# A product's difference of weight blocks, kept from its first use instead of loaded three times

## The chip, the core and the metric

The kernel runs on one NeuronCore of a Trainium2 chip. A core has five engines that run side by side, each through its own instructions in order: TensorE (PE, matrix products, results into PSUM banks), VectorE (DVE) and ScalarE (ACT) for elementwise work, GpSimd (POOL) and SyncE (SP), which here issues most transfers. Sixteen DMA engines move the data of all queues. Engines wait for one another through semaphores. The metric is the time of one execution on the device in microseconds; shorter is better.

## What is computed

One layer of a decoder trunk over 1024 positions of width 2048, cut to what matters:

```
h = RMSNorm(x)
P = h @ W_in                        # all columns of all groups in one projection
A: gMLP gating     B: gated DeltaNet (8 heads, short conv on q, k, v, chunked delta rule)
C: attention to 256 memory tokens   # each times SiLU of its own columns of P
x = x + concat(A, B, C) @ W_out
y = RMSNorm(x)
```

Everything is float32. A float32 product is made from three products of faster type: each operand is split into a high part and a rest, and high x high, high x rest and rest x high are added.

## The kernel before

**A planner sets the order.** The kernel's text doesn't issue its instructions at once. `Plan.add` (line 138) records each with its operands, a rank and the instructions it depends on. `Plan.issue` (line 229) then plays them through with the kernel's own fixed costs (for example a fixed latency for a transfer, line 67, and a further one for GpSimd's, line 204) and writes out an order for every engine: whatever is ready goes by rank, small numbers first, then by place in the program. So each engine's order, fixed before the program runs, follows from the whole list of instructions. `behind(op)` holds an instruction back until `op` is done. Matrix products of the projection have rank 9 and fill TensorE wherever nothing more urgent is ready; weight and operand loads have rank 4, splits into high part and rest have rank 2, subtractions of blocks rank 2 (`minus`, line 1397), the steps of the early inverse rank 3 (line 1280).

**Two parts of the projection.** The first half of the DeltaNet heads is projected plainly, head by head (`project`, line 861). The rest of P, and the output projection, use Strassen-Winograd products: a pair of 512 column blocks and the two halves of the positions make a 2x2 problem with the two halves of the 2048 rows of W, and seven products of blocks are made instead of eight (`seven`, line 1340). There are five column pairs of W_in (`pairs`, line 740; `project_pair`, line 1460) and two of W_out. Each product m is made in four chunks of two 128-row blocks; a chunk is 24 matmuls of 128x512 with two operands that are loaded, combined and split. The order of the products of a pair is 2, 1, 6, 5, 3, 7, 4 (line 1337).

**The operands.** The left ones (`h_left`, line 1378) are loaded from DRAM, sums and differences being made earlier. The right ones are made from weight blocks B(i, b): half i of the rows, column block b. With T = B(0,1) - B(0,0), product 1 takes B(0,0), product 6 takes B(1,1) - T, product 5 takes T itself, product 3 takes B(1,1) and turns the kept T into B(1,1) - T, and products 7 and 4 use that. `rights_made` (line 1430) does it. `plain` loads a pair of 128x512 blocks into one of three raw tiles (`wraw2`, line 1302; the trace calls them `wraw` or `y`), `load2` loads into given tiles. The tiles in which T is kept are eight of 128x512, two per chunk (`kept`, line 1305): slots of the rings that the trace calls kT, qT, kd and ai, which an earlier part of the DeltaNet work used.

**What runs beside the first pair.** The first column pair (C_Q and C_K of the later heads) starts when the plain projection ends. At the same time the DeltaNet work of the early heads goes on. It needs inverses of 32x32 triangular blocks (`inverse`, line 995): 62 small steps on VectorE and one copy, then GpSimd sends the result to DRAM (`tdrearly`, `udrearly`), reads it back in pieces into `tblk` and `ut` (`levels`, line 1022), and small matmuls combine the pieces. Then the scan over chunks follows, interleaved with the products.

**The first pair is an exception.** In `rights_made` the flag `late` is set for pair 0 alone. There the kept tiles aren't filled in product 1. Product 6 loads B(0,1) into two of the `yz` tiles and B(0,0) into a raw tile, and makes T in `yz`; product 5 loads both again and makes T in the kept tiles.

Of the kernel before, what the change touches and what calls it, by code (L numbers as in the profile page):

```python
# [22 lines left out]
HT = 512  # L23
# [37 lines left out]
class Plan:  # L61
# [27 lines left out]
    @contextmanager  # L89
    def rank(self, cls):  # L90
        old, self.cls = self.cls, cls
        yield
        self.cls = old

    @contextmanager
    def behind(self, op):
        old, self.gate = self.gate, op
        yield
        self.gate = old
# [204 lines left out]
def kernel(  # L304
# [115 lines left out]
    def main_bank():  # L420
        turn["acc"] += 1
        return acc[turn["acc"] % 2]
# [45 lines left out]
    def triple(a, l, r, start, stop, cls=9):  # L468

        mm(a, l[0], r[0], start, False, cls)  # L470
        mm(a, l[0], r[1], False, False, cls)
        return mm(a, l[1], r[0], False, stop, cls)
# [194 lines left out]
    for mt in range(2):  # L667
        t = [ring["ai"](F32R) for _ in range(2)]
# [9 lines left out]
    for h in range(NX):  # L678
        t = ring["vs"](F32R).rearrange("p (s m) -> p s m", s=2)
# [68 lines left out]
    def blk(w, k, c0):  # L748
        return w[k * P : (k + 1) * P, c0 : c0 + HT]
# [547 lines left out]
    yu, yz, obs = ([t[:, k * HT : (k + 1) * HT] for k in range(4)] for t in ywide[:3])  # L1297
# [7 lines left out]
    kept = [[ring[tag](slot=k) for k in range(2)] for tag in ("kT", "qT", "kd", "ai")]  # L1305
# [7 lines left out]
    wide = [main_bank(), main_bank()] + acc[2:4]  # L1313
# [3 lines left out]
    def load2(ts, src):  # L1317

        for i, x_ in enumerate(src):
            t = ts[i] if len(ts) == 2 else ts[0][:, i * HT : (i + 1) * HT]  # L1320
            Q.dma_start(t, x_)
        return ts
# [9 lines left out]
    def add(o, a, b, cls=1):  # L1332
        with rank(cls):
            V.tensor_tensor(out=o, in0=a, in1=b, op=ALU.add)


    ORDER, FIRST, SUM = (2, 1, 6, 5, 3, 7, 4), (1, 7, 2), {5: 0, 6: 1, 7: 2, 3: 3}
    ends, chunk_ends = {}, [marks[-1]] * 8

    def seven(left, right, banks, takes, order, rows=False, last=False):  # L1340


        for n, key in enumerate(order):
            c, m = divmod(key, 10)
            bank = banks(key)

            def product(t, i, a, w):
                for u in range(2):
                    mine, whole = slice(u * HT + t * P, u * HT + (t + 1) * P), slice(u * HT, (u + 1) * HT)
                    l, r, ls, rs = (a, w, mine, whole) if rows else (w, a, mine, whole)  # L1350
                    triple(bank[t], (l[0][:, ls], l[1][:, ls]), (r[0][:, rs], r[1][:, rs]),
                           i + u == 0 and m in FIRST, i + u == NH - 1)

            held = []
            for i in range(0, NH, 2):
                js = (i, i + 1)
                a, w = left(m, js), right[c](m, js)
                if last and key == order[-1] and i >= NH - 6:
                    held.append((i, a, w))
                else:  # L1360
                    for t in range(NT):
                        product(t, i, a, w)
                    chunk_ends.append(R.ops[-1])
                    if todo and len(chunk_ends) % 4 == 0:
                        with behind(R.ops[-1]), rank(3):
                            todo.pop(0)()
            for t in range(NT):
                for h in held:
                    product(t, *h)
                ends[key, t] = R.ops[-1]  # L1370
                takes[key](t, bank[t])
# [16 lines left out]
    def plain(srcs):  # L1388
        with rank(4):
            return load2([wraw2()], srcs)[0]  # L1390

    def split_r(srcs):
        return split2(srcs, whi3(), wlo3())
# [3 lines left out]
    def minus(o, a, b):  # L1397
        with rank(2):
            V.tensor_tensor(out=o, in0=a, in1=b, op=ALU.subtract)
# [27 lines left out]

        return get

    def rights_made(blocks, late=False):  # L1430

        def get(m, js):
            n = js[0] // 2
            ts = yz[n % 2 * 2 :][:2] if late and m == 6 else kept[n]
            if m in ((6, 5) if late else (1,)):
                with rank(4), behind(chunk_ends[-8]):
                    load2(ts, [blocks(0, 1, j) for j in js])
                if late:  # L1440
                    r = plain([blocks(0, 0, j) for j in js])
                    for i, t in enumerate(ts):
                        minus(t, t, r[:, i * HT : (i + 1) * HT])
            if m == 5:
                return split_r(ts)
            r = plain([blocks(*AT[m], j) for j in js])
            parts = [(t, r[:, i * HT : (i + 1) * HT]) for i, t in enumerate(ts)]
            if m < 4:
                w = split_r([r])
                if m == 3 or m == 1 and not late:  # L1450
                    for t, x_ in parts:
                        minus(t, *((t, x_) if m == 1 else (x_, t)))
                return w
            for t, x_ in parts:
                minus(x_, *((t, x_) if m == 7 else (x_, t)))
            return split_r([r])

        return get

    def project_pair(c, done, dest=None):  # L1460


        def keep(o, a):
            with rank(1):
                S.copy(o, a)

        def fin(hf, b, t, a, y=None):
            o = dest(hf, t) if dest and b == 1 else ob()
            if y is None:
                keep(o, a)  # L1470
            else:
                add(o, a, y)
            with rank(2.4):
                done(hf, b, t, o)

        takes = {
            2: lambda t, a: keep(yu[t], a),
            1: lambda t, a: fin(0, 0, t, a, yu[t]),
            6: lambda t, a: keep(yz[t], a),
            5: lambda t, a: keep(yu[t], a),  # L1480
            3: lambda t, a: fin(0, 1, t, a),
            7: lambda t, a: fin(1, 1, t, a, yu[t]),
            4: lambda t, a: fin(1, 0, t, a, yz[t]),
        }

        def w_block(i, b, j):
            return blk(w_in, NH * i + j, pairs[c][b])

        seven(h_left, [rights_made(w_block, c == 0)], lambda m: wide, takes, ORDER)

    def to_conv(which):
        def done(hf, t, y):
# [4 lines left out]
    def blocks(c, *dones, dest=None):  # L1497
        project_pair(c, lambda hf, b, t, y: dones[b](hf, t, y), dest)
# [145 lines left out]
    for n, (tag, to) in enumerate((("gt", mkT), ("inv", mv))):  # L1644
        for i in range(NX // 2):
            t = ring[tag](F32R).rearrange("p (h s m) -> p h s m", h=2, s=2)
# [106 lines left out]
    takes, rights = {}, []  # L1753

    def out_pair(cp):
# [42 lines left out]
        def w_block(i, b, j):  # L1798
            return blk(w_out, (set1, set2)[i][j], (c1 + b) * HT)

        rights.append((rights_made, rights_back)[cp](w_block))

    out_pair(0)
# [33 lines left out]
```

## Time and profile before

| | |
|---|---|
| runs | 1626.72 us median of 3 (1624.07 to 1627.04) |
| profiled execution | 1629.2 us, span of its instructions 1627.2 us |
| granted TensorE clock, mean | 0.997 |
| VectorE / ScalarE / GpSimd busy | 1268.3 / 1025.2 / 277.4 us |
| moved by DMA | 428.92 MB, mean 264 GB/s |

In the profile's rows all instructions carry line 300, since the planner issues them from there; work is told apart by tile names, which leave out buffer numbers (`y` is any of the tiles y0 to y3, among them `yz`, and the third raw tile). `out<-in,in` names what an instruction writes and reads. A row of waits reads: waiting engine and tile <- what ended the wait: total us, times, longest. A row of DMA issues ends in the count, the size of one, and the median us from issue to landing. A matmul that is shown as busy is pipelined with the next one: 24 matmuls of 128x512 follow one another at about 0.22 us.

### The profile page before, as it was taken

What the parts mean: (1) busy time and instruction counts of PE and PEld (TensorE: products, weight loads), DVE (VectorE), ACT (ScalarE), POOL (GpSimd) and SP (SyncE); (2) the same over time, 40 slices, a digit from 0 to 9 for tenths busy, and PEclk for the clock granted to TensorE, in tenths of its full rate; (3) what the DMA queues carried; (4) which work ended last, traced back from release to release, by engine and by line L of the source; (5) the groups of instructions that cost most, each with busy time, mean ns of one, the idle gap of its engine ahead of it and who ended that gap; (6) DMA issues with size and microseconds to landing.
All of it is one profiled execution on the core that took longest, in us unless ns stands there. A gap on an engine that the chain in (4) does not pass through costs nothing.

```text
span 1627.2 us, 26085 instructions
## 1 busy us (share of the span) xinstructions
PE 1611.0 (99%) x8576; PEld 1354.4 (83%) x8576; DVE 1268.3 (78%) x2119; ACT 1025.2 (63%) x2216; POOL 277.4 (17%) x466
## 2 busy tenths in 40 slices
PE   9999999999999999999999999999999999999997
PEld 8988888888888888888888888888888888888886
DVE  6866787869855567898998898778668888679875
ACT  7767675765456555888787444776757774345355
POOL 0011220360252210112222502223100000000001
PEclk9999999999999999999999999999999999999999
DMA  9866998888967975689868976898768879688646
GB/s 326 245 197 193 305 303 260 277 255 309 369 204 256 308 242 182 209 279 364 289 215 279 350 243 204 256 340 262 253 221 271 290 246 371 202 267 294 222 150 235
DMA packets 277129, 428.92 MB, mean 264 GB/s; under 512 B 30665, under 2 KB 102402, under 8 KB 276994
## 3 DMA queue, kind: packets, MB, share of 16 engines
q1 hardware_dynamic: 254098, 366.75, 68.5%
q0 software_dynamic: 22144, 59.40, 10.9%
q8 instruction: 67, 1.10, 0.3%
q10 hardware_dynamic: 752, 1.12, 0.2%
q14 instruction: 68, 0.56, 0.1%
HBM read 339.57 MB, written 87.06 MB: 262 GB/s over the span
## 4 chain that ended last, share of the span: by engine, by line
PE 88%; DMA 4%; issue 3%; DVE 3%; ACT 1%; SPq 0%; POOL 0%; POOLq 0%; DVEq 0%; ACTq 0%
PE acc L300 66%; PE dn L300 22%; DMA wraw<-hTd 1%; DVE y L300 1%; DMA wraw<-in_w_in_dram 1%; DMA tdrearly<-inv 0%; DVE alo L300 0%; DVE wlo L300 0%; DMA vs<-od 0%; DMA raws<-h0d 0%; ACT ahi L300 0%; DVE tn L300 0%; DMA qT<-in_mem_dram 0%; DMA ut<-udrearly 0%; DMA tblk<-tdrearly 0%
## 5 line engine op out<-in xcount | busy, mean ns | idle before, releaser
L300 PE MATMUL acc<-ahi,whi 128*128 128x512 f32 (+1 forms) x1512 | 537.6, 393 | 0.1
L300 PE MATMUL acc<-ahi,wlo 128*128 128x512 f32 (+1 forms) x1144 | 447.8, 392 | 0.0
L300 PEld LDWEIGHTS acc<-ahi,whi 128*128 128x128 f32 x1512 | 283.3, 188 | 53.9 <-ACT xr L300 0.2
L300 PE MATMUL acc<-alo,whi 128*128 128x512 f32 (+1 forms) x776 | 302.1, 389 | 0.0
L300 PEld LDWEIGHTS acc<-ahi,wlo 128*128 128x128 f32 x1144 | 215.6, 188 | 41.3 <-DVE wlo L300 0.5
L300 ACT CAST whi<-wraw 128x512 fp32r<-128x512 f32 (+1 forms) x167 | 133.9, 803 | 123.7 <-PE acc L300 90.6
L300 DVE TENSOR_TENSOR wlo<-wraw,whi 128x512 fp32r<-128x512 f32 (+1 forms) x167 | 153.7, 921 | 70.7 <-ACT whi L300 67.6
L300 ACT CAST ahi<-raws 128x1024 fp32r<-128x1024 f32 x130 | 136.3, 1048 | 64.0 <-PE acc L300 25.5
L300 PEld LDWEIGHTS acc<-alo,whi 128*128 128x128 f32 x776 | 146.4, 189 | 27.5
L300 PE MATMUL acc<-ahi,zl 128*128 128x512 f32 x376 | 149.1, 396 | 0.0
L300 PE MATMUL acc<-alo,zh 128*128 128x512 f32 x376 | 148.7, 395 | 0.0
L300 PE MATMUL acc<-ahi,zh 128*128 128x512 f32 x376 | 148.1, 394 | 0.0
L300 POOL TENSOR_TENSOR small<-small,mhalf 128x1 f32<-128x1 f32 x26 | 15.6, 605 | 531.2 <-DVE small L300 524.7
L300 DVE TENSOR_TENSOR alo<-y,ahi 128x1024 fp32r<-128x1024 f32 x65 | 79.4, 1221 | 15.0 <-ACT ahi L300 14.6
L300 ACT CAST ahi<-y 128x1024 fp32r<-128x1024 f32 x65 | 68.1, 1047 | 36.4 <-PE dn L300 18.3
L300 DVE TENSOR_TENSOR alo<-raws,ahi 128x1024 fp32r<-128x1024 f32 x65 | 79.8, 1228 | 13.9 <-ACT ahi L300 13.8
L300 DVE TENSOR_TENSOR ahi<-raws,ahi 128x1024 fp32r<-128x1024 f32 x65 | 79.4, 1221 | 13.2 <-ACT ahi L300 13.0
L300 PEld LDWEIGHTS acc<-alo,zh 128*128 128x128 f32 x376 | 70.7, 188 | 13.7
L300 PEld LDWEIGHTS acc<-ahi,zh 128*128 128x128 f32 x376 | 70.8, 188 | 13.6
L300 PEld LDWEIGHTS acc<-ahi,zl 128*128 128x128 f32 x376 | 70.8, 188 | 13.5
L300 PE MATMUL acc<-whi,ahi 128*128 128x512 f32 x232 | 79.9, 392 | 0.0
L300 PE MATMUL dn<-whi,ahi 128*128 128x512 f32 x216 | 74.2, 389 | 0.0
(423 smaller groups left out, 3397.6 us busy)
## 6 DMA issues: line engine op xcount, KB each, us to landing
wraw<-in_w_in_dram SPq DMA_DIRECT2D x268, 256.0 KB, 4.2
raws<-sd SPq DMA_DIRECT2D x150, 256.0 KB, 4.0
y<-in_w_in_dram SPq DMA_DIRECT2D x92, 256.0 KB, 3.7
y<-sd SPq DMA_DIRECT2D x75, 256.0 KB, 3.9
wraw<-in_w_out_dram SPq DMA_DIRECT2D x64, 256.0 KB, 4.1
raws<-h0d SPq DMA_DIRECT2D x54, 256.0 KB, 5.9
y<-in_w_out_dram SPq DMA_DIRECT2D x33, 256.0 KB, 4.6
sd<-zg SPq DMA_DIRECT2D x32, 256.0 KB, 4.2
```

The lines of the kernel that those rows point to most:

```text
L300: o.fn(*o.args, **o.kw)
```

## The change

The flag `late` goes. Pair 0 fills the kept tiles in product 1 like the other four pairs: there B(0,1) is loaded into them, and B(0,0), which product 1 loads for itself, is subtracted. Product 6 then subtracts the kept T from B(1,1), and product 5 splits the kept T. The additional loads of B(0,1) and B(0,0) in products 6 and 5 go, and `yz` is no longer used for T.

```diff
-    def rights_made(blocks, late=False):
+    def rights_made(blocks):
         def get(m, js):
             n = js[0] // 2
-            ts = yz[n % 2 * 2 :][:2] if late and m == 6 else kept[n]
-            if m in ((6, 5) if late else (1,)):
+            ts = kept[n]
+            if m == 1:
                 with rank(4), behind(chunk_ends[-8]):
                     load2(ts, [blocks(0, 1, j) for j in js])
-                if late:
-                    r = plain([blocks(0, 0, j) for j in js])
-                    for i, t in enumerate(ts):
-                        minus(t, t, r[:, i * HT : (i + 1) * HT])
             if m == 5:
                 return split_r(ts)
...
                 w = split_r([r])
-                if m == 3 or m == 1 and not late:
+                if m in (1, 3):
                     for t, x_ in parts:
                         minus(t, *((t, x_) if m == 1 else (x_, t)))
                 return w
...
-        seven(h_left, [rights_made(w_block, c == 0)], lambda m: wide, takes, ORDER)
+        seven(h_left, [rights_made(w_block)], lambda m: wide, takes, ORDER)
```

## The prediction

> **What bounds the kernel now.** I read the page's first part, then TensorE's waits, then a table of windows around the first column pair, then the chain of waits through that stretch, and last the DMA issues there.
>
> ```profile
> span 1627.2 us, 26085 instructions
> PE 1611.0 (99%) x8576; PEld 1354.4 (83%) x8576; DVE 1268.3 (78%) x2119; ACT 1025.2 (63%) x2216; POOL 277.4 (17%) x466
> ```
>
> TensorE (PE) is busy 99% of the span. So an edit that takes no matrix product away can gain no more than TensorE loses in waits. All waits of TensorE are these:
>
> ```profile
> PE dn L300 <- DMA ut<-udrearly: 2.0, 1, 2.0
> PE dn L300 <- DMA qT<-in_mem_dram: 2.0, 1, 2.0
> PE dn L300 <- POOL ones L300: 1.1, 1, 1.1
> PE acc L300 <- DVE tn L300: 0.8, 1, 0.8
> PE dn L300 <- DVE ai L300: 0.8, 1, 0.8
> PE acc L300 <- ACT gt L300: 0.5, 1, 0.5
> ```
>
> The waits for qT, ones and gt belong to the start of the program, which the change doesn't reach. Of the others one alone lies in the stretch that the change edits: 2.0 us for `ut<-udrearly`. The next table (columns: window, length, busy time and count of PE, weight loads, DVE, ACT, POOL, then granted clock, DMA share, GB/s) covers the pair's first products: about 364 to 397 us is product 2, 397 to 419 product 1, 419 to 441 product 6, then 5. I placed the borders by the evictions of each product's four banks; the first of product 2 and the first of product 1 are these (start, length):
>
> ```profile
> 396.14 0.58 ACT L300 COPY y<-acc 128x512 f32<-128x512 f32 x1
> ...
> 419.38 0.68 DVE L300 TENSOR_TENSOR y<-acc,y 128x512 f32<-128x512 f32 x1
> ```
>
> ```profile
> 364.00:397.00 33.00, 33.00 (x151) 27.29 (x151) 30.49 (x58) 18.89 (x30) 4.56 (x10) 1.00 0.88 304
> 397.00:419.00 22.00, 22.00 (x99) 18.23 (x98) 20.12 (x38) 9.66 (x11) 0.00 (x0) 1.00 0.98 347
> 419.00:441.00 22.00, 22.00 (x99) 18.23 (x98) 19.35 (x28) 7.27 (x9) 5.84 (x10) 1.00 1.03 384
> 441.00:470.00 29.00, 27.04 (x239) 22.01 (x239) 20.75 (x34) 15.32 (x35) 13.07 (x23) 0.94 0.84 254
> ```
>
> In the first three rows TensorE has no idle time at all, though DMA is full (0.98 and 1.03) and VectorE (DVE) nearly so. In the fourth it loses 29.00 - 27.04 = 2.0 us and some clock. The finer windows (PE busy and count, clock, DMA share, GB/s) show where:
>
> ```profile
> 448.70:450.90 2.20, 0.24 (x4) 1.00 1.08 340
> 452.20:455.60 3.40, 3.40 (x10) 0.50 1.03 316
> ```
>
> After the idle 2.0 us the granted clock is 0.50 for 3.4 us, with ten matmuls started; at the pace of the 397 row (22.00 / 99 = 0.222 us) ten take 2.2 us. So this one wait costs 2.0 + (3.4 - 2.2) = 3.2 us, 0.2% of the time. The chain of waits says what it hangs on:
>
> ```profile
> 391.91 36.51 issue x2
> 428.44 7.55 DMA tdrearly<-inv
> 436.27 5.15 DMA tblk<-tdrearly
> 444.96 5.89 DMA ut<-udrearly
> 450.89 0.69 PE dn L300 x39
> ```
>
> The 36.51 us is time in which GpSimd (POOL) waited for VectorE to finish the early 32x32 inverses; then three small transfers follow one another, and TensorE meets the last of them. These run while the pair's weight loads fill the DMA engines.
>
> **The change part by part.** Products are counted by their number m; a chunk is a quarter of a product (two row blocks of weights), 24 matmuls.
>
> TensorE: the same 672 matmuls of the pair, none added or removed: 0.
>
> DMA loads. Before, product 6 loads block (0,1) into `yz` and (0,0) into a raw tile, and product 5 loads (0,1) into the kept tiles and (0,0) again: per chunk 4 + 4 loads, so 32. After, product 1 loads (0,1) into the kept tiles, 8 loads, and uses the (0,0) that it has. That is 24 loads fewer, and 8 (those into kT, qT, kd, ai) moved some 30 us forward past the queue of SyncE's other loads and stores.
>
> ```profile
> y<-in_w_in_dram SPq DMA_DIRECT2D x20, 256.0 KB, 5.5
> kT<-in_w_in_dram SPq DMA_DIRECT2D x2, 256.0 KB, 5.3
> ai<-in_w_in_dram SPq DMA_DIRECT2D x2, 256.0 KB, 5.2
> ```
>
> ```profile
> L300 SPq DMA_DIRECT2D y<-in_w_in_dram x20: 327/374/867, 374.8 to 435.0; - x20
> ```
>
> 24 x 256 KB = 6.3 MB, at 384 GB/s 16 us of full DMA. Directly it is worth 0, because TensorE in the 397 and 419 rows waits for none of it. Stage by stage, with the left operand's 8 loads per product, product 6 falls from 32 loads to 16 (8.4 MB to 4.2 MB in 22 us: 381 to 191 GB/s, where the trace has 384) and product 5 from 24 to 8. Issue time on SyncE's queue falls by 24 x 0.374 us (the median of the last row, min/median/max in ns) and hides likewise.
>
> The 8 moved loads come earlier: 2.1 MB, at the 304 GB/s of the first row 6.9 us of DMA, where (1 - 0.88) x 33 = 4.0 us are spare. If they delay the loads of product 2, TensorE waits up to 6.9 us; if they fit between, 0. I take 0: they have the same rank as the others but stand behind product 2's loads in the program, and their first reader that TensorE needs is product 6. No buffer holds them back either: the kept tiles' earlier contents leave for DRAM by this row, 80 us before.
>
> ```profile
> 314.60 0.61 POOL L300 DMA_DIRECT2D late<-kd  x1
> ```
>
> VectorE: 16 subtractions in products 6 and 5 go, 8 come in product 1. Directly -8 x 0.687 = -5.5 us, hidden, since TensorE doesn't wait. What counts is the inverse: 62 small VectorE steps of the lowest rank in this stretch, which fill in between the splits.
>
> ```profile
> L300 DVE TENSOR_TENSOR y<-y,wraw 128x512 f32<-128x512 f32 x4 | 2.7, 687 | 1.3 <-DMA wraw<-in_w_in_dram 1.3
> L300 DVE TENSOR_TENSOR y<-y,y 128x512 f32<-128x512 f32 x4 | 2.7, 686 | 0.0
> 427.94 1.16 DVE L300 COPY inv<-inv 128x1024 f32<-128x1024 f32 x1
> 428.91 1.22 DVE L300 TENSOR_TENSOR wlo<-wraw,whi 128x1024 fp32r<-128x1024 f32 x1
> ```
>
> Up to the end of the inverse (its copy at 427.94) the removed kind has run six times: all four `y<-y,wraw` and two of the `y<-y,y`. The new eight all lie before that point. So the inverse ends (8 - 6) x 0.687 = 1.4 us later, or 8 x 0.687 = 5.5 us later if none of the removed six would have been ahead of it; on the other side, 1.3 us of VectorE idling for a raw tile goes. I take +1.4. Behind a new subtraction that waits for its load, the splits and the inverse's steps queue on VectorE, and TensorE waits for the splits; the cover is the earlier load.
>
> The three transfers. The same kinds in the full stretch (425 to 455 us):
>
> ```profile
> wraw<-in_w_in_dram SPq DMA_DIRECT2D x11, 256.0 KB, 6.9
> ut<-udrearly POOLq DMA_DIRECT2D x8, 32.0 KB, 5.8
> tblk<-tdrearly POOLq DMA_DIRECT2D x7, 16.0 KB, 5.3
> ```
>
> and just after it (456 to 500 us, mean 208 GB/s), with the late inverse's copy at 998 us last:
>
> ```profile
> DMA packets 4559, 9.14 MB, mean 208 GB/s; under 512 B 848, under 2 KB 1070, under 8 KB 4554
> wraw<-in_w_in_dram SPq DMA_DIRECT2D x4, 256.0 KB, 4.4
> ut<-udrearly POOLq DMA_DIRECT2D x4, 32.0 KB, 3.4
> tblk<-tdrearly POOLq DMA_DIRECT2D x10, 16.0 KB, 3.8
> tdrlate<-inv POOLq DMA_DIRECT2D x1, 512.0 KB, 5.1
> ```
>
> At the low load the chain shortens by (5.8 - 3.4) + (5.3 - 3.8) = 3.9 us, with the first transfer (7.6 to 5.1) by 6.4 us; at an unchanged load by 0. The stage's own demand after the change, 191 GB/s, is nearest to the 208 row, so I take 3.9. With the inverse 1.4 us later the data arrives 2.5 us earlier against the same place in TensorE's order, more than the 2.0 us of the wait. The wait and its half clock go: -3.2 us. The ends are -3.2 (nothing more to gain here) and +5.5 with one more half-clock stretch of 1.2, +6.7.
>
> The clock is the place for a rule of the Trainium skill: TensorE: Matmul & The Clock Gate, Part 1, says the array falls to half rate after an idle window of about 3.4 us. By that rule a 2.0 us wait would not halve the clock and its removal would save 2.0 alone, a time 1.2 us above mine; here the trace has the half clock right behind the 2.0 us, and I go by the trace.
>
> The order. A planner in the kernel lays out all engines' orders from its own costs, so everything behind the first changed load is drawn anew. Nothing in the trace prices that; below zero it can remove the one 0.8 us wait left in that part, above it can make new ones.
>
> ```profile
> 747.20 0.39 PE L300 MATMUL dn<-inv 128*128 128x256 f32 x1 [0.77 <-DVE ai L300]
> ```
>
> I charge one new wait of that size, +0.8: in 1,250 us before, the redrawn part and its neighbourhood hold two of 0.8 us and the one of 2.0.
>
> Sum: 0 - 3.2 + 0.8 = -2.4 us. The profiled execution took 1629.2 us, 2.0 more than its span and 2.5 more than the median of 1626.72; it would become 1626.8, and the median 1624.3.
>
> **The rivals.**
> - Faster still: the wait with its half clock goes, nothing takes its place, and the 0.8 us at 747 goes too: -4.0, 1622.7 us. For it: DMA relief of half in the stage. Against: it needs a redrawn order without one new wait in 900 us.
> - No effect: the planner, which prices these transfers by constants and doesn't see the load, draws TensorE's step as much earlier as the data comes, or puts other loads into the free DMA time. 1626.7 us. Against: the raw tiles are few, so loads can't run far ahead.
> - Slower: the inverse ends 5.5 us later because its steps have the lower rank in product 1, where VectorE is at 20.12 of 22.00. Then TensorE waits 7.5 us at the `ut` step: +6.7, 1633.4 us. It decides as soon as the inverse's delay exceeds the transfers' gain minus 2.0 us. For it: VectorE has only 1.9 us to spare in that row.
> - Slower at the front: the moved loads go ahead of those of products 2 and 1, TensorE waits 6.9 us and loses 1.2 by the clock, less the 3.2 gained: +4.9, 1631.6 us. It decides where 6.9 us of loads meet 4.0 us of spare DMA. Against: their place in the program.
>
> **How the numbers follow.** About 0.2%, 3.3 us, is what a measurement of this kernel can tell from no change. Forecast 0.30, no effect 0.10, together 0.40 for the same; faster still 0.27; the late inverse 0.20 and the front 0.13, together 0.33 for slower. The time is the likeliest's, 1624.3 us; its own range is 1623 to 1627. The 8-in-10 range reaches from 1621 (below the faster case by about as much as runs of one kernel scatter) to 1633, just under the late inverse.
>
> **What would show it.** Right: the 397 to 450 us stretch at a DMA share well under 0.98, landing of `tblk` and `ut` near 4 us, no PE wait for `ut<-udrearly`, no half clock there; the inverse's copy at about 429 us; TensorE still at 99%. The prediction is wrong if that copy ends several us later, if PE waits for a split or raw tile between 376 and 420 us, or if new PE waits stand behind 500 us.

## The result

| | before | changed |
|---|---|---|
| median | 1627.04 us of 7 runs (1624.07 to 1631.03) | 1630.88 us of 7 runs (1629.09 to 1633.65) |
| ratio to before | | 1.0029, 95% interval 1.0017 to 1.0041 |
| the changed kernel again, 11 runs beside 27 of before | 1626.78 us | 1629.10 us, ratio 1.0018, interval 1.0009 to 1.0027 |

The changed kernel is slower by about 0.2 to 0.3%, 3 to 5 us by the ratios. (The ratios come with the runs and are not the quotients of the medians shown, which are 1.0024 and 1.0014, or 3.8 and 2.3 us; all say slower.) The forecast was 2.4 us faster. The profiled execution of the changed kernel took 1629.09 us, and its span of 1627.2 us equals that of the profiled execution of before by chance: it is the fastest of the changed kernel's first seven, and the one of before lies 2.2 us above its median. The whole spans of these two profiles therefore don't show the difference; their stretches do.

The first part of the page of the changed kernel:

```profile
span 1627.2 us, 26042 instructions
PE 1610.6 (99%) x8576; PEld 1353.8 (83%) x8576; DVE 1262.4 (78%) x2111; ACT 1024.2 (63%) x2214; POOL 284.9 (18%) x466
DMA packets 273673, 422.63 MB, mean 260 GB/s; under 512 B 30281, under 2 KB 102018, under 8 KB 273538
```

The change did what it says: 428.92 - 422.63 = 6.3 MB less is moved, VectorE has 8 instructions and 5.9 us less, TensorE the same 8576 matmuls. The stretch that was edited (the windows of the prediction, same columns):

```profile
364.00:397.00 33.00, 33.00 (x151) 27.33 (x150) 31.07 (x57) 18.36 (x29) 4.60 (x11) 1.00 0.96 329
397.00:419.00 22.00, 22.00 (x98) 18.21 (x97) 19.15 (x32) 9.07 (x10) 0.00 (x0) 1.00 0.76 245
419.00:441.00 22.00, 21.96 (x97) 17.76 (x96) 21.52 (x38) 9.57 (x12) 4.50 (x8) 1.00 0.88 294
441.00:470.00 29.00, 29.00 (x232) 24.05 (x231) 15.20 (x22) 16.67 (x33) 12.57 (x23) 1.00 0.58 174
```

The DMA share falls from 0.98 to 0.76, from 1.03 to 0.88 and from 0.84 to 0.58. In the first row it rises to 0.96, which fits the eight loads moved forward, and TensorE still loses nothing there. The last row has no idle time and no half clock any more. In the whole edited stretch TensorE is idle for 0.04 us. The waits of TensorE over the whole program:

```profile
PE dn L300 <- DVE tn L300: 2.8, 1, 2.8
PE dn L300 <- ACT E L300: 1.3, 1, 1.3
PE dn L300 <- POOL ones L300: 1.1, 1, 1.1
```

The others are of 0.7 us or less. The wait for `ut<-udrearly` is gone, and two that before did not have stand in its place: 2.8 us for `tn` and 1.3 us for `E`. Both lie far behind the edit, near 1000 and 1303 us. Windows around the first, and VectorE's instructions there (start, length, instruction, in brackets the idle time before it and what ended that):

```profile
994.00:1000.60 6.60, 6.60 (x36) 5.61 (x35) 1.12 (x2) 3.94 (x9) 1.56 (x3) 1.00 1.09 346
1000.60:1003.70 3.10, 0.42 (x2) 0.00 (x0) 1.83 (x3) 0.90 (x2) 0.00 (x0) 1.00 0.62 177
1003.70:1007.10 3.40, 3.26 (x10) 2.77 (x11) 3.37 (x5) 2.01 (x5) 0.00 (x0) 0.54 0.31 84
```

```profile
1000.53 0.69 DVE L300 TENSOR_TENSOR ai<-wraw,ai 128x512 f32<-128x512 f32 x1 [5.48 <-DMA wraw<-in_w_in_dram]
1002.49 0.69 DVE L300 TENSOR_TENSOR ai<-wraw,ai 128x512 f32<-128x512 f32 x1 [1.27 <-DMA wraw<-in_w_in_dram]
1003.10 0.68 DVE L300 SCALAR_TENSOR_TENSOR tn<-tn,tn 128x512 f32<-128x512 f32 x1
```

And the chain of waits through the same place:

```profile
992.22 1.24 DVE wlo L300
...
993.47 0.33 SPq L300
...
993.86 8.61 DMA wraw<-in_w_in_dram
...
1002.49 0.07 DVE ai L300
...
1003.10 0.69 DVE tn L300
...
1003.84 1.03 PE dn L300 x4
```

Read together: two subtractions of weight blocks (of a later column pair, which the change doesn't touch) wait on VectorE for a raw tile whose loads take up to 8.61 us, at a DMA share of 1.09. VectorE works in order, so the step `tn<-tn,tn` of the DeltaNet work, which needs nothing from that load, stands behind them, and TensorE stands behind `tn`. After it the clock is at 0.54 for 3.4 us, with ten matmuls started. At the 0.222 us each of the prediction's working, the place costs 2.8 + (3.4 - 2.2) = 4.0 us. The place at 1303 us has a similar form, here with a subtraction of the output projection ahead of a reciprocal:

```profile
1301.36 0.69 DVE L300 TENSOR_TENSOR kT<-kT,wraw 128x512 f32<-128x512 f32 x1 [1.80 <-DMA wraw<-in_w_out_dram]
1303.15 0.69 DVE L300 TENSOR_TENSOR kT<-kT,wraw 128x512 f32<-128x512 f32 x1 [1.09 <-DMA ai<-in_w_out_dram]
1303.76 0.16 DVE L300 RECIPROCAL small<-small 128x2 f32<-128x2 f32 x1
```

So there are two theories (the recorded expectations call the second one 'stage'). **Order:** the edit is good or harmless in its place, and the loss comes from the order that the planner draws behind it, in which block subtractions with late loads stand ahead of steps that TensorE needs. **Edit:** the loss comes from the edit's own loads, subtractions or the later inverse.

To see where an execution gains or loses, I divided it at three matmuls that every kernel has. A is the last with the tile `abw`, at 253.9 us before and 253.6 us after, ahead of any difference between the kernels. B is the first `dn<-wsT,el`, C the last `dn<-xb,inv`. The three of before and then of the changed kernel (count, shortest/median/longest ns, first to last start):

```profile
L300 PE MATMUL acc<-alo,abw x32: 389/396/476, 78.1 to 253.9; 128*128 128x512 f32 x32
L300 PE MATMUL dn<-wsT,el x8: 273/275/276, 947.5 to 948.3; 128*128 128x128 f32 x8
L300 PE MATMUL dn<-xb,inv x3: 392/395/398, 1349.2 to 1349.6; 128*128 128x512 f32 x3
```

```profile
L300 PE MATMUL acc<-alo,abw x32: 389/396/476, 77.5 to 253.6; 128*128 128x512 f32 x32
L300 PE MATMUL dn<-wsT,el x8: 273/275/275, 942.2 to 943.0; 128*128 128x128 f32 x8
L300 PE MATMUL dn<-xb,inv x3: 392/395/398, 1350.4 to 1350.9; 128*128 128x512 f32 x3
```

From A to B, which holds the edited stretch, the changed kernel takes 688.6 us in place of 693.6, 5.0 less. From B to C, which the edit doesn't reach, it takes 408.7 in place of 402.2, 6.5 more; behind C it has 276.3 in place of 277.5. The gain was there and was given back. The same three points serve all experiments below.

### The profile page after: what moved, and what is told of

The parts are those of the page before. It is cut to its first block, busy times and chain, and to the rows that moved or that the text cites. A ratio compares the mean times of both kernels' runs of the same rounds, so it can differ in the third digit from the quotient of the medians.

```text
span 1627.2 us, 26042 instructions
## 1 busy us (share of the span) xinstructions
PE 1610.6 (99%) x8576; PEld 1353.8 (83%) x8576; DVE 1262.4 (78%) x2111; ACT 1024.2 (63%) x2214; POOL 284.9 (18%) x466
## 2 busy tenths in 40 slices
DMA packets 273673, 422.63 MB, mean 260 GB/s; under 512 B 30281, under 2 KB 102018, under 8 KB 273538
## 4 chain that ended last, share of the span: by engine, by line
PE 92%; DMA 3%; DVE 2%; ACT 1%; issue 1%; SPq 0%; POOLq 0%; POOL 0%; ACTq 0%; DVEq 0%
PE acc L300 72%; PE dn L300 20%; DMA wraw<-in_w_in_dram 1%; DMA wraw<-hTd 1%; DVE wlo L300 0%; ACT whi L300 0%; DVE alo L300 0%; DMA kd<-in_x_dram 0%; DMA ai<-in_w_out_dram 0%; ACT ahi L300 0%; DMA qT<-in_mem_dram 0%; DMA wraw<-in_w_mem_kv_dram 0%; ACT jk L300 0%; SPq L300 0%; ACT tn L300 0%
## 6 DMA issues: line engine op xcount, KB each, us to landing
wraw<-in_w_in_dram SPq DMA_DIRECT2D x256, 256.0 KB, 4.1
raws<-sd SPq DMA_DIRECT2D x150, 256.0 KB, 3.7
y<-in_w_in_dram SPq DMA_DIRECT2D x80, 256.0 KB, 4.3
y<-sd SPq DMA_DIRECT2D x75, 256.0 KB, 3.9
wraw<-in_w_out_dram SPq DMA_DIRECT2D x64, 256.0 KB, 4.5
raws<-h0d SPq DMA_DIRECT2D x54, 256.0 KB, 5.2
y<-in_w_out_dram SPq DMA_DIRECT2D x33, 256.0 KB, 4.2
sd<-zg SPq DMA_DIRECT2D x32, 256.0 KB, 4.0
```

## The experiments

Medians and ratios of each run are against the kernel before on the same chip in the same series of runs.

**The changed kernel again.** No edit.

> The changed kernel again, for a second execution's trace. Theory 'order': the stretch of the first column pair is faster than before, and the loss sits behind it, where the planner has drawn the order anew: a TensorE wait of 2 to 4 us at about 1000 us behind a late raw tile, with a half-clock stretch, and perhaps one at 1303 us; ratio to before 1.002 to 1.004. Theory 'stage': the loss sits between 364 and 470 us (late splits or a late inverse), and the wait at 1000 us comes and goes between executions; same ratio.

Measured: 1629.10 us, ratio 1.0018 (1.0009 to 1.0027). TensorE waits 2.4 us for `tn` until 1007.6 us, with half clock from 1008.7; no wait near 449 us. A to B 690.4, B to C 406.6 us. The new wait near 1000 us is there in both executions. The one at 1303 us is not; in its place 1.1 us for `ahi` stand near 853 us.

**The kernel before again**, as a control.

> The kernel before again, a control. Both theories: ratio 1.000, within 0.001 of it; TensorE's wait for ut<-udrearly at about 449 us is there again, 1.5 to 3 us, with half a clock behind it.

Measured: 1626.94 us, ratio 1.0003 (0.9993 to 1.0014). The wait for `ut<-udrearly` is there again with 2.0 us. A to B 691.9, B to C 402.9 us.

**The edit in the old order.** The planner lays out before's 32 loads and 16 subtractions as it did. All 32 loads and all 16 subtractions are then left out when the order is written, and the 8 loads and 8 subtractions of the change are put in at a planned cost of nothing. TensorE's order is that of before, matmul by matmul.

```diff
+            if late and m == 1:
+                with rank(4.5), behind(chunk_ends[-8]), R.only("extra"):
+                    load2(ts, [blocks(0, 1, j) for j in js])
             if m in ((6, 5) if late else (1,)):
+                with R.only("drop" if late else "kept_all"):
...
+                if late and m == 1:
+                    with R.only("extra"):
+                        for t, x_ in parts:
+                            minus(t, t, x_)
...
-        for o in self.ops:
+        for o in [o for o in self.ops if not o.drop]:
```

> The change's loads and subtractions, but every engine's order of all other work as in the kernel before (the planner still plans the loads that are gone; they are only not issued). Theory 'order': the wait at 449 us goes as in the changed kernel and nothing comes in its place, so 1627.0 - 3.2 = 1623.8 us, ratio 0.998. Theory 'stage': the loss stays, about 1631 us, ratio 1.003.

Measured: 1633.11 us, ratio 1.0037 (1.0024 to 1.0049). Waits and the window of product 1:

```profile
PE acc L300 <- DVE alo L300: 3.8, 1, 3.8
```

```profile
397.00:419.00 22.00, 18.19 (x73) 14.56 (x72) 21.59 (x35) 8.17 (x10) 0.00 (x0) 0.92 0.62 203
```

By the ratio alone this would speak for 'stage'. The trace shows where the time goes, on VectorE:

```profile
394.62 0.69 DVE L300 TENSOR_TENSOR qT<-qT,y 128x512 f32<-128x512 f32 x1 [3.83 <-DMA y<-in_w_in_dram]
...
398.75 1.22 DVE L300 TENSOR_TENSOR zl<-wraw,zh 128x1024 fp32r<-128x1024 f32 x1
399.88 1.22 DVE L300 TENSOR_TENSOR alo<-y,ahi 128x1024 fp32r<-128x1024 f32 x1
```

The new subtractions `qT<-qT,y` wait for a raw tile of product 1 that SyncE issued behind the moved loads, and the splits that TensorE needs next stand behind them. ScalarE had made the high parts of these operands by 394.4 us, so the operands were there; TensorE was idle for 3.8 us until the split `alo` was done, and ran at half clock after it. It is a slowdown in the place of the prediction's rival "slower at the front". In the changed kernel the moved loads for qT, kd and ai go out ahead of that raw tile too, but there `qT<-qT,y` stands behind the splits (at 396.56 us), and TensorE loses nothing (33.00 of 33.00 and 22.00 of 22.00 us above). This run says nothing yet on the rest of the edit, except that the wait at 449 us went.

**The same with the moved loads later**, behind product 2's loads.

```diff
-                with rank(4.5), behind(chunk_ends[-8]), R.only("extra"):
+                with rank(4.5), behind(chunk_ends[-4]), R.only("extra"):
```

> As the run before it with the old order, but each chunk's two moved loads are issued only when TensorE has done the same chunk of product 2, so they stand behind the loads of product 2 that TensorE needs first. Theory 'order' (the edit by itself gains, the redrawn order loses): no wait near 397 us, none at 449 us, 1626.8 - 3.2 = 1623.6 us, ratio 0.998. Theory 'front' (the moved loads and subtractions cost TensorE time wherever they stand in products 2 and 1): a wait of 1 to 4 us between 380 and 420 us stays, ratio 1.000 or more.

Measured: 1626.29 us, ratio 0.9998 (0.9988 to 1.0009), and in a second series 1625.62 us, ratio 0.9992 (0.9983 to 1.0001):

> The change's loads and subtractions in the order of before, the moved loads behind product 2's loads, a second time: what the change is worth where the order does not move. Theory 'local gain' (the wait at 449 us and its half clock, 3.2 us by the prediction): 1622.5 to 1624.5, ratio 0.9975 to 0.999. Rival 'no gain' (before's wait at 449 us is paid back within the next stages): 1626.5, ratio 1.000, as the first run had it (0.9998).

The window from 441 to 470 us in the second series:

```profile
441.00:470.00 29.00, 29.00 (x299) 24.17 (x298) 17.78 (x30) 17.80 (x45) 11.96 (x22) 1.00 0.65 191
```

No wait stands at 397 or at 449 us, and between 441 and 470 us TensorE gains 3.8 us against each of the first two profiles of before (its order is the same, so the starts compare one by one). Yet by the ratios the gain is only 0.3 and 1.3 us, and the first median is even 0.5 us above before's 1625.79 of its series. The expectation of about 3 us was missed, and why is taken up again below. No loss by the edit itself is seen: A to B 689.0 and 687.8, B to C 402.4 and 402.9 us.

**The redrawn order without the edit.** In the kernel before, the planner alone is told that the early inverse's copy comes out 2.2 us, or 3.3 us, later. No instruction is added, removed or changed; the order behind that point is drawn anew.

```diff
-            V.tensor_copy(gd.rearrange("p i m -> p m i"), ti)
+            V.tensor_copy(gd.rearrange("p i m -> p m i"), ti).lat = 3300.0 if n == "early" else 0.0
```

> The kernel before with one number of its planner changed: the copy at the end of the early inverse is told to come out 2.2 us later, by which TensorE's step at 449 us is placed later and everything behind it is drawn anew; no instruction is added or taken away. Theory 'order': the wait at 449 us goes (-3.2 us), and what the redrawn order adds behind it is as large as in the changed kernel or larger, anything from 1624 to 1633 us. Theory 'stage' (the order hardly matters): 1623.6 us, ratio 0.998.

> The same with 3.3 us: a second redrawn order of the unchanged instructions. Theory 'order': the wait at 449 us goes, and the sum differs from the run with 2.2 us by 2 us or more, since other waits are made and unmade. Theory 'stage': as with 2.2 us, 1623.6 us, ratio 0.998.

Measured: 1630.90 us, ratio 1.0026 (1.0016 to 1.0036), and 1629.72 us, ratio 1.0023 (1.0015 to 1.0032). The waits of TensorE in the second:

```profile
PE dn L300 <- DVE tn L300: 2.6, 1, 2.6
PE dn L300 <- ACT E L300: 0.7, 1, 0.7
```

and its chain of waits at the first of these:

```profile
994.64 8.37 DMA y<-in_w_in_dram
...
1003.04 0.07 DVE ai L300
...
1003.65 0.69 DVE tn L300
...
1004.39 0.66 PE dn L300 x4
```

Without any edit to the work the same wait stands at the same place, behind the same late load (8.37 us, in the changed kernel 8.61), and the time rises by as much as the change did. B to C takes 410.0 and 406.2 us, as in the changed kernel. The theory "edit" is not needed for the loss. Two parts of the expectations failed. The wait for `ut` near 449 us is still there in the profile with 2.2 us, with 1.4 us and a half clock (that profile is of the slowest of its 11 runs, 1636.97 us, and has the wait for `tn` too, with 2.8 us). And the two orders differ by 1.2 us, not by 2 or more.

**One VectorE step moved in the changed kernel.** Behind the planner, before the order is written, the two subtractions `ai<-wraw,ai` are put behind the step `tn<-tn,tn`. Every other engine's order stays.

```diff
+        by[9680].at = by[9681].at = by[8199].at + 0.5
         self.ops.sort(key=lambda o: (o.at, o.idx))
```

> The changed kernel with one VectorE step moved: at about 1000 us the step that makes the tile tn, for which TensorE waits, stands before the two subtractions that wait for the late raw tile, not behind them. Theory 'order': the 2.8 us wait and its half clock (3.4 us with some 1.4 lost) go, 1630.9 - 4.2 = 1626.7 us, ratio 1.000. Theory 'stage': no change against the changed kernel, 1631 us, ratio 1.003.

Measured: 1626.61 us, ratio 0.9998 (0.9988 to 1.0008), where the changed kernel in the same series has 1.0018. The wait for `tn` and its half clock are gone; B to C falls from 406.6 to 403.6 us. In this profile 1.6 us for `ahi` stand near 853 us. One pair of instructions, moved on an engine that is busy 78% of the time, carries the loss, as far as the intervals can tell.

**The same move in the redrawn order without the edit** (3.3 us).

```diff
+        by[9712].at = by[9713].at = by[8231].at + 0.5
```

> The kernel before with the planner's copy price 3.3 us later (no instruction changed, order redrawn; 1629.72 us, ratio 1.0023), and in that order the two ai<-y,ai subtractions moved behind tn<-tn,tn on VectorE near 1000 us. Theory 'order': the wait of 2.6 us for tn goes, as it went in the changed kernel, and with it most of the loss: 1626 to 1627.5, ratio 0.9998 to 1.0008. Rival (the loss lies elsewhere in the redrawn order): the wait goes and the ratio stays at 1.002.

Measured: 1627.32 us, ratio 1.0003 (0.9994 to 1.0013), down from 1.0023. Two windows over the place, first without and then with the move:

```profile
985.00:1010.00 25.00, 22.42 (x180) 18.61 (x172) 15.25 (x22) 14.94 (x33) 8.80 (x15) 1.00 0.80 252
```

```profile
985.00:1010.00 25.00, 25.00 (x206) 21.06 (x205) 15.78 (x24) 15.62 (x35) 10.79 (x19) 1.00 0.83 256
```

The idle 2.6 us go, as forecast, and most of the loss with them. (A wait of 1.1 us for `ut<-udrearly` near 450 us stands in this execution.)

**Three such moves in the changed kernel**: as above, and the same for `wraw<-kT,wraw` near 853 us and `kT<-kT,wraw` near 1303 us.

```diff
+        for k, j in ((9680, 8199), (9681, 8199), (7766, 5847), (7767, 5847), (11716, 11217), (11717, 11217)): by[k].at = by[j].at + 0.5
```

> The changed kernel with VectorE subtractions of the block products moved behind the step that TensorE waits for, at three places in place of one: ai<-wraw,ai behind tn<-tn,tn (1000 us, as in the run before with one move), wraw<-kT,wraw behind kT<-tn,kT (near 853 us) and kT<-kT,wraw behind the reciprocal and xa<-vs,xa (near 1302 us). Nothing else changes. Theory 'order' (the loss is late block loads on VectorE's in-order queue ahead of steps that TensorE waits for): the waits of 1.1 to 1.6 us near 853 us and of 1.5 us near 1303 us go too, the time falls by the one move's 2 to 4 us and by 1 to 2.5 more: 1624 to 1626, ratio to before 0.998 to 0.9995. Rival 'spread' (the redrawn order loses a little at many places that no wait shows, or a wait that is taken away comes back behind it): the waits go and the time stays at that of the one move, 1626.6, ratio 1.000. If the loss were none of these waits: 1629, ratio 1.002.

Measured: 1624.96 us, ratio 0.9990 (0.9981 to 0.9999); span of the profiled execution 1621.7 us. VectorE at the place of the first move:

```profile
999.56 0.69 DVE L300 SCALAR_TENSOR_TENSOR tn<-tn,tn 128x512 f32<-128x512 f32 x1 [4.04 <-ACT tn L300]
1000.23 0.69 DVE L300 TENSOR_TENSOR ai<-wraw,ai 128x512 f32<-128x512 f32 x1
1001.78 0.69 DVE L300 TENSOR_TENSOR ai<-wraw,ai 128x512 f32<-128x512 f32 x1 [0.86 <-DMA wraw<-in_w_in_dram]
```

The load is still late (the second subtraction waits for it, until 1001.78), but `tn` is done 3.5 us earlier than in the changed kernel, and TensorE has no wait above 1.1 us left in the whole program, nor any near 853 or 1303 us. (The profile is of the fastest of its 11 runs.) A to B 689.1, B to C 402.7, behind C 276.3 us, from A to the end 5.4 us less than the changed kernel's first profile. This version has the lowest ratio measured here, 0.1% under before, with an interval that only just excludes no change. It overlaps those of the one move (0.9998) and of the edit in the old order (0.9992), so what the two further moves add is not shown.

**Is the wait at 449 us always there?** Two further profiles of the kernel before, to explain why the edit in the old order gains 3.8 us at this place in the profiles and about 1 us by the ratios.

> The kernel before, one more profiled execution: is the wait for ut<-udrearly near 449 us there in every execution? In both profiled ones so far it cost about 3.8 us between 441 and 470 us (wait and half clock) against the change in the old order, yet that version's median is only 0.3 to 1.3 us under before's. Theory 'sometimes': the wait depends on how the transfers fall and is absent, or under 1 us, in many executions: then in one of two further profiles too. Theory 'always': it is there again with 2.0 us, and the difference of the medians lies in the first 250 us, which vary by 4 us between executions before any difference of the kernels (time of the last decay matmul 252.6 to 256.9 us).

> The same as the run before it, a fourth profile of the kernel before. 'Sometimes': the stretch from 441 to 470 us shows TensorE busy for over 28 of 29 us and full clock in one of the two. 'Always': 27 of 29 us and a clock of 0.94 in both, as in the first profile.

Measured: 1622.39 and 1623.76 us, one run each, beside one of before with 1625.70. The window from 441 to 470 us in the first and in the second:

```profile
441.00:470.00 29.00, 28.98 (x306) 24.38 (x305) 21.59 (x36) 18.61 (x46) 12.93 (x23) 1.00 0.75 232
```

```profile
441.00:470.00 29.00, 28.16 (x296) 23.45 (x295) 21.04 (x36) 17.67 (x43) 12.50 (x22) 1.00 0.78 239
```

In the first the wait is absent, in the second it is 0.8 us and the clock stays at 1.00. So it is there in full in two of four executions of the same program. The first transfer behind the inverse, `tdrearly<-inv`, goes with it: it took 7.55 and 7.27 us in the executions with the full wait, 6.5 and 6.6 us in these two. A to B is 693.6 and 691.9 us in the executions with the wait, 688.0 and 689.5 us in these two. Against these two, the edit in the old order gains only 0.2 to 0.3 and 1.1 us between 441 and 470 us: it gains the wait where the wait is, and little else.

This does not explain all of the small gain. Half of 3.8 us is 1.9 us, and from A to the end the edit in the old order is 1.8 us faster on the mean of its two profiles against the four of before. But it reaches A later (256.2 and 255.7 us) than any of the four (252.6 to 253.9), though all engines' instructions up to A and their order are the same. Whether that is chance or belongs to the kernel stays open.

All profiled executions but that of the edit in the old order with early loads (A at 255.4, A to B 696.7, B to C 401.7 us), from the starts of A, B and C and the spans (C to end agrees within 0.1 us in a row):

| kernel | A at | A to B | B to C | C to end |
|---|---|---|---|---|
| before, four profiles | 253.9, 252.6, 252.9, 253.2 | 693.6, 691.9, 688.0, 689.5 | 402.2, 402.9, 401.9, 401.5 | 277.5 |
| edit in old order, later loads, two profiles | 256.2, 255.7 | 689.0, 687.8 | 402.4, 402.9 | 277.5 |
| changed, two profiles | 253.6, 256.0 | 688.6, 690.4 | 408.7, 406.6 | 276.3 |
| redrawn without the edit, 2.2 and 3.3 us | 256.0, 253.7 | 692.8, 689.3 | 410.0, 406.2 | 276.3 |
| the 3.3 us one with one move | 256.9 | 690.0 | 404.2 | 276.3 |
| changed with one move, with three | 256.3, 253.5 | 692.0, 689.1 | 403.6, 402.7 | 276.3 |

The column B to C separates the orders: 401.5 to 402.9 us in all six profiles of the old order in this table, with the edit or without, and 406.2 to 410.0 us in all four of the redrawn one, with the edit or without, until the subtractions are moved.

## Why the prediction was wrong

The step that failed is "The order", charged with +0.8 us. It measured about +4 us: +0.0026 and +0.0023 of 1626 us are 4.2 and 3.7 us, with no edit at all. I had priced it by the waits that the order of before holds, 0.8 us each, over the redrawn part. But those waits are what is left in an order as it stands; they say little about a new one from the same planner. The planner gives each transfer a fixed latency, the load at 994 us took 8.61 us at a DMA share of 1.09, and so a subtraction that was planned as ready was not. The price of such a miss is not the size of the old waits. It is the lateness of a load, as far as what stands behind it on an in-order engine feeds TensorE, and a half clock may come on top. In hindsight the prediction had rows for a bound: landings of 6.9 us in the full stretch and 4.4 us after it are 2.5 us of lateness, with 1.2 us for the clock 3.7 us for one place, in place of 0.8. It also had the mechanism, for the edited stretch alone ("behind a new subtraction that waits for its load, the splits and the inverse's steps queue on VectorE"), and did not carry it to the part that is drawn anew. It even named "new PE waits behind 500 us" as what would make it wrong, but gave them no rival and no chance of their own.

The second step that was mis-sized is the gain of -3.2 us. Its mechanism was right: the loads fall, the stage's DMA share falls from 0.84 to 0.58, the wait and its half clock go, and 3.8 us were gained against an execution that has the wait. But I took one profiled execution for all of them. The wait is there in full in two of four, which fits a mean gain of about half of that; the ratios have 0.3 to 1.3 us, and the rest is open, as said above. The profiled execution stood 2.5 us above the median, and I treated that as a constant to subtract; it may have been in part the very wait that I was pricing (the other execution with the full wait, 1626.87 us, lies at the median).

- TensorE's work 0, DMA and VectorE directly 0: right. 6.3 MB and 5.9 us of VectorE went, and the one wait of TensorE that went in the edited stretch is that for `ut`.
- The moved loads, 0 taken, 6.9 us as the bound: right for the changed kernel. The edit in the old order with early loads lost about as much as the bound, 6.8 us (against the profile of before its matmuls are 1.6 us late at 384 us and 8.4 us at 404 us). But that was VectorE's order, not the lack of DMA time from which the bound was worked out, so that the sizes agree may be luck.
- The inverse +1.4 us: wrong both ways. In the old order the copy comes no later (173.4 and 171.5 us behind A, before 172.3 to 174.0). In the redrawn one it does by 5.7:

```profile
433.31 1.14 DVE L300 COPY inv<-inv 128x1024 f32<-128x1024 f32 x1
451.20 0.69 PE L300 MATMUL dn<-tblk,gt 32*32 32x32 f32 x32
```

 That is 179.7 us behind A against 174.0, past the bound of 5.5. The planner had also put TensorE's first `tblk` product later, it starts at 451.20 us in place of 444.90, so nobody waited. The rival "late inverse" had the delay right and its effect wrong: TensorE's place is drawn along with the delay.
- The three transfers, 5.1, 3.8 and 3.4 us forecast for the first, `tblk` and `ut`: right. (In the old order, at a DMA share of 0.65 between 441 and 470 us, they are 5.5 to 6.0, 3.3 to 3.6 and 4.0 to 4.3 us.) From 425 to 455 us of the changed kernel:

```profile
tdrearly<-inv POOLq DMA_DIRECT2D x1, 512.0 KB, 4.2
ut<-udrearly POOLq DMA_DIRECT2D x8, 32.0 KB, 3.3
tblk<-tdrearly POOLq DMA_DIRECT2D x7, 16.0 KB, 3.9
```

- "Faster still" needed a redrawn order without a new wait in 900 us; the nearest to it here is the order with the three moves, and it gives -0.1%.

So the sum that the ratios give is -0.3 to -1.3 us for the edit and about +4 us for the order, near +3 us; the two measurements of the change are +0.0018 and +0.0029 of 1627 us, 2.9 and 4.7 us. Why the planner puts those subtractions ahead of `tn` in the redrawn order and not in that of before was not traced further than its fixed costs. What remains of the B to C difference behind the named waits of the first profile (6.5 - 4.0 - 1.3 = 1.2 us) is not assigned to places.

## What to carry to other kernels

In a kernel whose order is drawn by a planner, price an edit in two parts: the edit itself in the old order, and a redrawn order with no edit; here the second was several times the first and had the other sign. A redrawn order costs what a late load costs where it stands on an in-order engine ahead of a step that the bounding engine needs, so look for such pairs and move the load's consumer behind. Before a single wait is priced from a profile, see in further executions whether it is there at all: the second one here still had it in full.

## What the runs showed of the hardware

- A wait that hangs on a chain of transfers under full DMA comes and goes between executions of one program: 2.0, 2.0, 0 and 0.8 us in four of the kernel before, while TensorE's time from B to C agrees within 1.4 us in the same four.
- The executions differ most before anything else happens: A falls between 252.6 and 256.9 us in 14 profiles although the instructions ahead of it are the same. The 60th matmul starts between 12.6 and 17.4 us, and the wait for `qT<-in_mem_dram` near the start is 0 to 2.7 us.
- A wait of 2.0 us was followed by a half clock in both profiles of before that have it, and the 2.8 us one of the changed kernel by 0.54 for 3.4 us, but the 2.6 us wait of the redrawn order (3.3 us) by none: its window from 985 to 1010 us, above, has a clock of 1.00. In the redrawn order with 2.2 us a wait of 1.4 us was followed by 3.4 us at half clock and one of 2.8 us by some 6.8 us, while waits of 0.8 us (the fourth profile of before) and 1.1 us (for `ut`, in the 3.3 us order with one move) were followed by none. The Trainium skill, TensorE: Matmul & The Clock Gate, Part 1, describes a window of about 3.4 us that runs freely, not started by the work. The length of the stretch, 3.4 us, and that equal waits are or are not followed by it agree with that; that an idle window of the whole 3.4 us is needed does not, since 1.4 us were enough here.
